# Moving part of the last gate's adaLN rows from the first product of an MLP into its second, as half rows through the weight loads' buffers

## The chip, the cores and the metric

The kernel runs on 1 core of one Trainium2 chip. The metric is device time in microseconds (us), the median over runs of one program. Before the change three runs took 1998.12, 2001.72 and 2003.39 us, so the median is 2001.72. One more execution was recorded by the profiler: it took 2001.01 us, with a span of 1999.3 us between its first and last recorded instruction.

The engines are named as the profile names them: PE multiplies matrices, DVE does elementwise arithmetic and sums along rows, ACT applies functions and copies, POOL and SP issue DMA transfers (SP issues most of them, in program order).

## The reference, cut to what matters

One decoder layer on x of shape (1, 512, 2048) in float32. A conditioning vector c gives six vectors of 2048 numbers, and the last of them, `gt2`, scales what the MLP adds at the end:

```python
c_act = jax.nn.silu(c.astype(jnp.float32))
mod = (c_act @ w_ada[l].astype(jnp.float32) + b_ada[l]).reshape(B, N_MOD, D)
sh1, sc1, gt1, sh2, sc2, gt2 = [mod[:, j][:, None, :] for j in range(N_MOD)]
# ... attention and a recurrence, then:
h = rmsnorm(x, g_norm_mlp[l]).astype(jnp.float32) * (1.0 + sc2) + sh2
hid = jnp.square(jax.nn.relu(jnp.einsum('bsd,df->bsf', h, w_mlp_in[l].astype(jnp.float32))))
y = jnp.einsum('bsf,fd->bsd', hid, w_mlp_out[l].astype(jnp.float32))
x = (x.astype(jnp.float32) + gt2 * y).astype(x.dtype)
```

`gt2` is a product of a vector of 2048 numbers with a 2048 x 2048 part of `w_ada`. It needs nothing but c and the weights, and it is needed first where the first 512 columns of the second MLP product are finished.

## The kernel before

All activations lie transposed, 128 features by 512 tokens to a tile. Each matrix product in float32 is made of three matmuls on operands that are split into a high and a low part (`h`, `lo`); the split of a weight is a copy on ACT (the high part) and a subtraction on DVE (the low part, line 122).

**The two MLP products** use one level of a Strassen scheme (function `strassen`): seven products of half-size blocks instead of eight. The work comes in *sets*. A set is one 512 KB weight load, the sums that Strassen needs of it, and 42 matmuls of 128 x 256 (seven products, two halves, three matmuls each; lines 1100 to 1102). The first product (8192 hidden features, 16 groups of 512) runs from group 1 on as 8 sets each; the second (`parts`, 13 pieces) has 124 sets of the same shape. In each set, function `operands`:

- SP loads the weights into one of three buffers with the tag `raw` (line 1056);
- DVE adds blocks of them (lines 1058, 1065, 1066) into a tile `ts`;
- ACT copies three raw blocks and the four sums into high parts (lines 1064 and 1070), and DVE subtracts for the low parts (line 122: `w<-raw` with 768 columns, `w<-ts` with 1024). The raw blocks' parts lie in six tiles `w3`, the sums' parts in five tiles (four `w4`, one `w5`), two tiles to a set. So the low part of a set's sums goes into the tile that held the high part of the set two before.

DVE and ACT execute in program order, and so does SP with its DMA issues. A raw buffer is free again when DVE's `w<-raw` of its set is done; the load three sets later waits for that on SP.

**Around the sets.** At the end of a group DVE combines the seven products from PSUM (`combine`, lines 1112 to 1118; ACT line 1111 copies the first one). In the first product DVE then makes four more sums of the result (line 946), ACT and DVE split it, and POOL writes all of it to DRAM (`keep_parts`). In the second product the results come back: five tiles of 256 KB for a set (`load_pair`, lines 1139 and 1142, on SP), and DVE finishes the split of two of five tiles (`split_pair`, line 122, `a<-a,a`). Those loads come in stretches, for four or eight sets on end. The time slots of `load_pair` and `split_pair` are set by the table `todo`.

**The rows of `gt2`** are made by `ada_late(GT2)`, a generator that runs beside the sets. It loads a quarter of 128 rows of the transposed `w_ada` (128 x 512, 256 KB, line 1190, on SP), and DVE multiplies it by the broadcast vector and sums along the row (line 1201, a SCALAR_TENSOR_TENSOR with a sum, followed by a DVE_READ_ACCUMULATOR); after four quarters two small operations (lines 1206 and 1207) add them into `mods`. That is 16 x 4 quarter rows. A generator in a `Lane` goes on when its `yield`s have counted down; `tick()` counts one for each set. Here `pace[0] = 1.9`, so a quarter row is due about every 1.9 sets, from group 2 on. The quarter rows lie in tiles with the tag `n` (five buffers, three loads ahead), the last two in tiles `a`. The list scheduler of the tile layer then places each instruction on its engine; instructions under `tc.high_priority` are moved ahead. Profile names drop buffer numbers, and both `w3`, `w4` and `w5` read `w` there.

Of the kernel before, what the change touches and what calls it, by code (L numbers as in the profile page):

```python
# [13 lines left out]
ALU = mybir.AluOpType  # L14
PSUM = bass.MemoryType.PSUM

P = 128
S = 512
D = 2048
NK = D // P  # L20
# [6 lines left out]
C_BADA = 0  # L27
# [37 lines left out]
def hybrid_layer_kernel(  # L65
# [13 lines left out]
    nc = tc.nc  # L79
# [18 lines left out]
    def T(tag, dt=F32, cols=None):  # L98
        return new(next(split_tag) if tag == "w4" else tag, dt, cols)
# [15 lines left out]
    tt = nc.vector.tensor_tensor  # L115
# [25 lines left out]
    cb = [T("cb"), T("cb")]  # L141
# [6 lines left out]
    def col(base, j):  # L148
        return vec[:, base + j : base + j + 1]
# [33 lines left out]
    def mod(m, j):  # L183
        return mods[:, m * NK + j : m * NK + j + 1]
# [256 lines left out]
    for o in range(8):  # L441
        t = T("a")
# [264 lines left out]
    pace = [3.2]  # L707
# [110 lines left out]
    def out_evac(outs, g, tok, held=None):  # L818
# [35 lines left out]
        out=gm2, in0=mods[:, SC2 * NK : (SC2 + 1) * NK], scalar=1.0, in1=vec[:, C_GMLP : C_GMLP + NK],  # L854
        op0=ALU.add, op1=ALU.mult,
# [325 lines left out]
        for f, p in todo.get(next(at), []):  # L1181
            f(p)

    LEAD, row = 3, ["n"]

    def ada_late(m):

        def load(i):
            t = T(row[0])
            tc.keep_in_program_order(nc.sync.dma_start(t, w_adaT[(m * NK + i // 4) * P : (m * NK + i // 4 + 1) * P, i % 4 * S : (i % 4 + 1) * S]))  # L1190
            return t

        ts = [load(i) for i in range(LEAD)]
        for i in range(4 * NK):
            t, q = ts.pop(0), i % 4
            if i + LEAD < 4 * NK:
                ts.append(load(i + LEAD))
            yield pace[0]
            if q == 0:
                ga = T("ga")  # L1200
            stt(
                out=t, in0=t, scalar=1.0, in1=cb[q // 2][:, q % 2 * S : (q % 2 + 1) * S], op0=ALU.mult, op1=ALU.mult,
                accum_out=ga[:, q : q + 1],
            )
            if q == 3:
                tt(out=ga[:, :2], in0=ga[:, :2], in1=ga[:, 2:4], op=ALU.add)
                stt(
                    out=mod(m, i // 4), in0=ga[:, 0:1], scalar=ga[:, 1:2], in1=col(C_BADA, m * NK + i // 4),
                    op0=ALU.add, op1=ALU.add,
                )  # L1210
        ready.add(m)

    pace[0] = 1.9
    w_pair = w_mlp_in.rearrange("(c k p) f -> k p c f", c=2, p=P)
    for g in range(1, NG):
        if g == 2:
# [8 lines left out]
        bg.add((keep_parts if g < NG - 2 else hold_parts)(g, *rs))  # L1225


    row[0] = "a"
    prodD = [[dp.tile([P, S], F32, name=f"prod_{n}_{i}") for i in range(7)] for n in range(NO)]
    w_blocks = w_mlp_out.rearrange("(g c b p) d -> g b p c d", c=2, b=2, p=P)  # L1230
    x2 = {}
# [235 lines left out]
```

## Time and profile before

| | before |
|---|---|
| median of three runs | 2001.72 us |
| the profiled execution | 2001.01 us |
| its span | 1999.3 us |
| PE busy | 1947.6 us (97%) |
| DVE busy | 1761.3 us (88%) |
| ACT busy | 1073.4 us (54%) |
| POOL busy | 193.6 us (10%) |
| granted PE clock, mean | 0.995 |
| DMA | 443.56 MB, 222 GB/s over the span |

Busy time counts an instruction from its start to its recorded end. Neighbours overlap on PE and DVE, so the time that one instruction costs is the distance between two starts, and the best measure of PE's progress is the number of matmuls that start in a stretch. In the span, the first MLP product's sets run from 764 to about 1363 us, the second product's until about 1959 us. Quarter rows run on DVE from 839.5 to 1359.2 us (62 of them), and two more after that.

### The profile page before, as it was taken

How to read it: one execution, taken by the hardware profiler on the slowest of the kernel's cores; microseconds unless marked ns; L12 is line 12 of the kernel's file. 1: busy time of each engine (PE TensorE's matmuls, PEld its weight loads, DVE VectorE, ACT ScalarE, POOL GpSimd, SP SyncE). 2: the span in 40 equal slices, each digit the busy share in tenths (PEclk: the TensorE clock that was granted, in tenths of full speed). 3: DMA queues.
4: the chain of work that ended last, by engine and by line, in shares of the span. 5: the costliest groups of instructions: out<-in, count | busy, mean ns of one | idle time of the engine just before them, and what ended most of it. 6: DMA issues, size and time to landing. Idle time of an engine off the chain costs nothing. (4 is left out here: it accounts for less than half of the span.)

```text
span 1999.3 us, 37951 instructions
## 1 busy us (share of the span) xinstructions
PE 1947.6 (97%) x14532; PEld 1836.1 (92%) x14532; DVE 1761.3 (88%) x2971; ACT 1073.4 (54%) x1572; POOL 193.6 (10%) x307
## 2 busy tenths in 40 slices
PE   8999999999999998999999999999999999999997
PEld 6789898788888898999999999999999999999996
DVE  8998786888998599999999999999879879878996
ACT  5443564786533386555556555555445645556552
POOL 0000000000000000111211211200110210211100
PEclk9999999999999999999999999999999999999998
DMA  9896655646779543766766765756567668679653
GB/s 365 305 319 213 201 169 183 188 140 213 228 251 362 183 144 113 236 211 196 227 201 191 227 204 187 232 170 219 190 232 270 226 246 287 215 253 346 225 196 111
DMA packets 205241, 443.56 MB, mean 222 GB/s; under 512 B 20481, under 2 KB 42113, under 8 KB 205058
## 3 DMA queue, kind: packets, MB, share of 16 engines
q1 hardware_dynamic: 176338, 356.58, 54.3%
q0 software_dynamic: 23680, 77.61, 10.4%
q10 hardware_dynamic: 5040, 6.93, 1.0%
q8 instruction: 114, 1.87, 0.4%
q14 instruction: 69, 0.57, 0.1%
HBM read 376.30 MB, written 64.75 MB: 221 GB/s over the span
## 5 line engine op out<-in xcount | busy, mean ns | idle before, releaser
L1100 PE MATMUL ps_mm<-a,w 128*128 128x256 f32 x1696 | 468.3, 277 | 3.0 <-DVE a L1112 1.2
L1102 PE MATMUL ps_mm<-a,w 128*128 128x256 f32 x1696 | 468.5, 277 | 0.4 <-DVE w L122 0.3
L1101 PE MATMUL ps_mm<-a,w 128*128 128x256 f32 x1696 | 468.3, 276 | 0.3 <-DVE a L122 0.3
L1070 ACT ACTIVATE w<-ts 128x1024 fp32r<-128x1024 f32 x244 | 258.4, 1059 | 276.2 <-DVE ts L1066 246.5
L1102 PE MATMUL ps_z<-a,w 128*128 128x256 f32 x1304 | 361.6, 278 | 7.0 <-DVE w L122 6.7
L1100 PE MATMUL ps_z<-a,w 128*128 128x256 f32 x1304 | 361.6, 278 | 3.8 <-DVE a L1116 1.7
L1101 PE MATMUL ps_z<-a,w 128*128 128x256 f32 x1304 | 360.9, 277 | 0.1
L122 DVE TENSOR_TENSOR w<-ts,w 128x1024 fp32r<-128x1024 f32 x244 | 298.4, 1223 | 54.7 <-PE ps_mm L1101 17.7
L1100 PEld LDWEIGHTS ps_mm<-a,w 128*128 128x128 f32 x1696 | 318.3, 188 | 4.3 <-issue 2.6
L1102 PEld LDWEIGHTS ps_mm<-a,w 128*128 128x128 f32 x1696 | 318.4, 188 | 1.2 <-DVE w L122 1.0
L1101 PEld LDWEIGHTS ps_mm<-a,w 128*128 128x128 f32 x1696 | 318.5, 188 | 0.7 <-DVE a L122 0.7
L122 DVE TENSOR_TENSOR w<-raw,w 128x768 fp32r<-128x768 f32 (+1 forms) x296 | 268.5, 908 | 37.1 <-ACT w L244 21.8
L1064 ACT ACTIVATE w<-raw 128x768 fp32r<-128x768 f32 x244 | 204.4, 838 | 168.4 <-issue 77.2
L1102 PEld LDWEIGHTS ps_z<-a,w 128*128 128x128 f32 x1304 | 245.6, 189 | 8.4 <-DVE w L122 8.3
L1100 PEld LDWEIGHTS ps_z<-a,w 128*128 128x128 f32 x1304 | 245.6, 188 | 5.4 <-issue 2.2
L1101 PEld LDWEIGHTS ps_z<-a,w 128*128 128x128 f32 x1304 | 245.6, 188 | 0.6 <-DVE a L122 0.6
L244 ACT ACTIVATE wh<-wr 128x512 fp32r<-128x512 f32 (+1 forms) x184 | 113.1, 618 | 151.3 <-PE ps_mm L262 62.4
L1058 DVE TENSOR_TENSOR ts<-raw 128x512 f32<-128x512 f32 x244 | 167.6, 688 | 14.1 <-DMA raw<-in_w_mlp_out_dram 13.6
L259 PE MATMUL ps_mm<-a,wh 128*128 128x512 f32 x448 | 176.3, 394 | 3.8 <-ACT wh L244 2.2
L263 PE MATMUL ps_mm<-a,wl 128*128 128x512 f32 x448 | 175.4, 392 | 0.8 <-DVE wl L122 0.6
L262 PE MATMUL ps_mm<-a,wh 128*128 128x512 f32 x448 | 174.8, 390 | 0.0
L211 DVE SCALAR_TENSOR_TENSOR x<-x,cb 128x1024 f32<-128x1024 f32 x108 | 131.8, 1224 | 25.0 <-DMA x<-in_w_adaT_dram 24.9
(336 smaller groups left out, 4156.7 us busy)
## 6 DMA issues: line engine op xcount, KB each, us to landing
raw<-in_w_mlp_out_dram SPq DMA_DIRECT2D x124, 512.0 KB, 4.7
raw<-in_w_mlp_in_dram SPq DMA_DIRECT2D x120, 512.0 KB, 3.9
x<-in_w_adaT_dram SPq DMA_DIRECT2D x108, 512.0 KB, 5.9
wr<-in_w_in_dram SPq DMA_DIRECT2D x160, 256.0 KB, 3.4
tt<-in_w_adaT_dram SPq DMA_DIRECT2D x52, 512.0 KB, 6.4
part<-a POOLq DMA_DIRECT2D x84, 256.0 KB, 3.9
a<-part SPq DMA_DIRECT2D x84, 256.0 KB, 6.4
prod<-a POOLq DMA_DIRECT2D x63, 256.0 KB, 5.7
```

Source lines behind the costliest of these rows:

```text
L122: tt(out=out, in0=full, in1=f32(high), op=ALU.subtract)
L211: ins = stt(out=t, in0=t, scalar=1.0, in1=cb[q_], op0=ALU.mult, op1=ALU.mult, accum_out=self.ga[:, q_ : q_ + 1],)
L244: act(h[:, :n], r[:, :n], AF.Copy)
L259: first = mm(out, wh, ah, start=start, stop=False, **kw)
L262: mm(out, wh, al, start=False, stop=False, **kw)
L263: mm(out, wl, ah, start=False, stop=stop, **kw)
L1058: tt(out=t[:, : 2 * HT].rearrange("p (a b) -> p a b", a=2), in0=r[:, HT : 3 * HT].rearrange("p (a b) -> p a b", a=2), in1=r[:, q_(0)].unsq ...
L1064: act(h, r[:, HT:], AF.Copy)
L1070: act(h, t, AF.Copy)
L1100: mm(out, wh[:, blk(i)], ah, start=st, stop=False, **kw)
L1101: mm(out, wh[:, blk(i)], al, start=False, stop=False, **kw)
L1102: mm(out, wl[:, blk(i)], ah, start=False, stop=j == js[-1], **kw)
```

## The change

The rows of `gt2` become due every 3.0 sets in place of 1.9. From the start of the second product on (`wide`), what is not yet loaded comes as half rows (128 x 1024, 512 KB, line 1197 of the changed file), one every 6 sets, in the three `raw` buffers of the weight loads and under the same priority as these; DVE works on a half row in one instruction (line 1207 of the changed file), about two sets after its load is placed.

```diff
-    LEAD, row = 3, ["n"]
+    LEAD, wide = 3, []
...
+        def load(n, at):
+            i, c0 = divmod(at, 2048)
+            src = w_adaT[(m * NK + i) * P : (m * NK + i + 1) * P, c0 : c0 + n]
+            if n == S:
+                t = T("n")
+                tc.keep_in_program_order(nc.sync.dma_start(t, src))
+            else:
+                with tc.high_priority(offset=SETW):
+                    t = T("raw")
+                    nc.sync.dma_start(t, src)
+            return t, n, at
...
+        def dot(t, n, at):
+            c0 = at % 2048
+            if c0 == 0:
+                used.clear()
+                used.append(T("ga"))
+            ga, q = used[0], len(used) - 1
+            used.append(n)
             stt(
-                out=t, in0=t, scalar=1.0, in1=cb[q // 2][:, q % 2 * S : (q % 2 + 1) * S], op0=ALU.mult, op1=ALU.mult,
+                out=t, in0=t, scalar=1.0, in1=cb[c0 // 1024][:, c0 % 1024 : c0 % 1024 + n], op0=ALU.mult, op1=ALU.mult,
                 accum_out=ga[:, q : q + 1],
             )
...
+        used, ts, at, end = [], [], 0, 2048 * NK
+        while at < end or ts:
+            while at < end and len(ts) < LEAD and not (wide and at % 1024 == 0):
+                ts.append(load(S, at))
+                at += S
+            if ts:
+                yield pace[0]
+                dot(*ts.pop(0))
+            else:
+                t = load(1024, at)
+                at += 1024
+                yield 2.0
+                with tc.high_priority(offset=SETW):
+                    dot(*t)
+                del t
+                yield 2 * pace[0] - 2.0
...
-    pace[0] = 1.9
+    pace[0] = 3.0
...
-    row[0] = "a"
+    wide.append(1)
```

In the built program this makes 40 quarter rows and 12 half rows (40 x 512 + 12 x 1024 = 16 x 2048 columns). All 40 quarter rows now stand on DVE before the last combination of the first product; before, 62 stood there and 2 after it. The orders of PE and ACT differ only around the end of the first product and, on ACT, by a few places of split copies in the second; POOL's is the same, and before group 2 and after the last half row nothing is moved.

On DVE, the end of group 3 of the first product, just ahead of its combination (the third L1112, into `ps_o`). `n` is a quarter row, `ga` its sums, `ts` and `w` belong to sets. Before:

```order
L1058 TENSOR_TENSOR ts_9520<-raw_9518 128x512
L946 TENSOR_TENSOR a_8981<-a_8981,a_9255 128x512
L1065 TENSOR_TENSOR ts_9520<-ts_9520,raw_9518 128x256
L1201 SCALAR_TENSOR_TENSOR n_8979,ga_9136<-n_8979,cb_82 128x512
L1066 TENSOR_TENSOR ts_9520<-ts_9520,raw_9518 128x256
L1206 TENSOR_TENSOR ga_9136<-ga_9136 128x2
L1201 SCALAR_TENSOR_TENSOR n_9138,ga_9654<-n_9138,cb_81 128x512
...
L1065 TENSOR_TENSOR ts_9592<-ts_9592,raw_9590 128x256
L1201 SCALAR_TENSOR_TENSOR n_9259,ga_9654<-n_9259,cb_81 128x512
L1066 TENSOR_TENSOR ts_9592<-ts_9592,raw_9590 128x256
L1201 SCALAR_TENSOR_TENSOR n_9378,ga_9654<-n_9378,cb_82 128x512
```

After:

```order
L1058 TENSOR_TENSOR ts_9507<-raw_9505 128x512
L1207 SCALAR_TENSOR_TENSOR n_9250,ga_9426<-n_9250,cb_82 128x512
L1065 TENSOR_TENSOR ts_9507<-ts_9507,raw_9505 128x256
L1207 SCALAR_TENSOR_TENSOR n_9428,ga_9426<-n_9428,cb_82 128x512
L1066 TENSOR_TENSOR ts_9507<-ts_9507,raw_9505 128x256
L1213 TENSOR_TENSOR ga_9426<-ga_9426 128x2
L1207 SCALAR_TENSOR_TENSOR n_9642,ga_10213<-n_9642,cb_81 128x512
...
L1058 TENSOR_TENSOR ts_9579<-raw_9577 128x512
L1214 SCALAR_TENSOR_TENSOR mods<-ga_9426,vec 128x1
L1065 TENSOR_TENSOR ts_9579<-ts_9579,raw_9577 128x256
L1066 TENSOR_TENSOR ts_9579<-ts_9579,raw_9577 128x256
```

Four quarter rows stood in the last two sets of this group, now three, and none in the last set. Up to this place stood 11 quarter rows, now 9; up to the end of group 4 it is 18 and 12. In each later group up to the 14th stood 4 or 5, now 2 or 3.

On SP, the first stretch of pair loads in the second product. Before:

```order
L1056 DMA raw_17788<-in_w_mlp_out_dram 128x2x512
L1139 DMA a_17652<-part_6510 128x512
L1142 DMA a_17656<-sum_6526 128x512
L1142 DMA a_17657<-sum_6526 128x512
L1139 DMA a_17716<-part_6510 128x512
L1056 DMA raw_17860<-in_w_mlp_out_dram 128x2x512
L1139 DMA a_17717<-part_6510 128x512
```

After, at the same pair loads:

```order
L1056 DMA raw_17714<-in_w_mlp_out_dram 128x2x512
L1139 DMA a_17578<-part_6510 128x512
L1142 DMA a_17582<-sum_6526 128x512
L1142 DMA a_17583<-sum_6526 128x512
L1139 DMA a_17642<-part_6510 128x512
L1197 DMA raw_17786<-in_w_adaT_dram 128x1024
L1139 DMA a_17643<-part_6510 128x512
L1139 DMA a_17644<-part_6510 128x512
L1142 DMA a_17648<-sum_6526 128x512
L1142 DMA a_17649<-sum_6526 128x512
L1056 DMA raw_17788<-in_w_mlp_out_dram 128x2x512
L1056 DMA raw_17860<-in_w_mlp_out_dram 128x2x512
```

The half row takes the place of a weight load, and this and every later weight load until the half row is used stand one raw buffer later.

On DVE at the same place, after the change (`a<-a,a` are the split subtractions; the first of them in this stretch stood right behind the same `ts<-raw` before):

```order
L122 TENSOR_TENSOR w_2969_17657<-raw_17652,w_2968_17656 128x768
L1058 TENSOR_TENSOR ts_17716<-raw_17714 128x512
L1207 SCALAR_TENSOR_TENSOR raw_17786,ga_17922<-raw_17786,cb_81 128x1024
L1065 TENSOR_TENSOR ts_17716<-ts_17716,raw_17714 128x256
L122 TENSOR_TENSOR a_17390<-a_17390,a_17708 128x512
L1066 TENSOR_TENSOR ts_17716<-ts_17716,raw_17714 128x256
L122 TENSOR_TENSOR a_17391<-a_17391,a_17711 128x512
L122 TENSOR_TENSOR w_2971_17663<-ts_17654,w_2970_17662 128x1024
```

The half row stands ahead of the rest of its set, and the next three sets hold two split subtractions each where the first two held three each and the third one. Of the twelve half rows two stand in this stretch (at its start and at its end) and two in the second stretch.

More of the change, by code (lines that the diff above doesn't have):

```diff
@@ L1182, in after_set @@
             f(p)
-    LEAD, row = 3, ["n"]
+    LEAD, wide = 3, []
     def ada_late(m):
[L1188 to L1200, printed above, removed]
+        def load(n, at):
[16 more added lines that the diff above has]
+            used.append(n)
@@ L1201, in ada_late @@
             stt(
-                out=t, in0=t, scalar=1.0, in1=cb[q // 2][:, q % 2 * S : (q % 2 + 1) * S], op0=ALU.mult, op1=ALU.mult,
+                out=t, in0=t, scalar=1.0, in1=cb[c0 // 1024][:, c0 % 1024 : c0 % 1024 + n], op0=ALU.mult, op1=ALU.mult,
                 accum_out=ga[:, q : q + 1],
             )
-            if q == 3:
-                tt(out=ga[:, :2], in0=ga[:, :2], in1=ga[:, 2:4], op=ALU.add)
+            if c0 + n == 2048:
+                if q > 1:
+                    tt(out=ga[:, : q - 1], in0=ga[:, : q - 1], in1=ga[:, 2 : q + 1], op=ALU.add)
@@ L1207, in ada_late @@
                 stt(
-                    out=mod(m, i // 4), in0=ga[:, 0:1], scalar=ga[:, 1:2], in1=col(C_BADA, m * NK + i // 4),
+                    out=mod(m, at // 2048), in0=ga[:, 0:1], scalar=ga[:, 1:2], in1=col(C_BADA, m * NK + at // 2048),
                     op0=ALU.add, op1=ALU.add,
                 )
+        used, ts, at, end = [], [], 0, 2048 * NK
[14 more added lines that the diff above has]
+                yield 2 * pace[0] - 2.0
```

## The prediction, as put on record before the change was run

> **What bounds the kernel now.** I read the page's totals first, then PE by stretches, then who PE waits for, then DVE's instructions one by one.
>
> ```profile
> span 1999.3 us, 37951 instructions
> PE 1947.6 (97%) x14532; PEld 1836.1 (92%) x14532; DVE 1761.3 (88%) x2971; ACT 1073.4 (54%) x1572; POOL 193.6 (10%) x307
> ```
>
> PE leaves about 52 us in all, and much of that lies where nothing is changed. In the windows view (span, then busy time and instructions of PE, PEld, DVE, ACT, POOL, clock, DMA share, GB/s) the third column's count is what to look at:
>
> ```profile
> 850.00:950.00 100.00, 97.22 (x836) 95.47 (x835) 98.80 (x179) 54.48 (x75) 17.00 (x25) 1.00 0.64 204
> 950.00:1150.00 200.00, 199.91 (x1763) 199.74 (x1763) 197.47 (x337) 111.19 (x146) 38.88 (x57) 1.00 0.66 212
> 1150.00:1350.00 200.00, 198.15 (x1740) 197.46 (x1740) 196.90 (x336) 110.03 (x148) 30.04 (x45) 1.00 0.62 198
> 1350.00:1400.00 50.00, 46.99 (x396) 45.64 (x395) 48.13 (x79) 30.22 (x44) 0.56 (x1) 1.00 0.61 218
> 1400.00:1480.00 80.00, 80.00 (x709) 80.00 (x708) 67.51 (x103) 38.06 (x47) 11.25 (x21) 1.00 0.49 166
> 1480.00:1530.00 50.00, 50.00 (x444) 50.00 (x443) 43.16 (x66) 26.74 (x36) 2.18 (x4) 1.00 1.00 370
> 1640.00:1690.00 50.00, 50.00 (x444) 50.00 (x443) 45.30 (x69) 28.43 (x38) 0.00 (x0) 1.00 0.95 342
> ```
>
> In the second product PE starts 709 matmuls in 80 us, 8.86 per us, without a gap: 42 of a set take 4.74 us. In the first product DVE is busy 98 to 99% and PE falls behind: 50 matmuls of 886 in the first row (5.6 us), 9 (1.0 us), 32 (3.6 us), and 48 (5.4 us) at the change of products. The first three sum to 10.2 us. So the first product has two engines at their limit, the second only PE. What PE waits for, from 840 to 1345 us and from 1345 to 1410 us:
>
> ```profile
> PE ps_z L1100 <- DVE a L1116: 1.7, 3, 0.6
> PE ps_mm L1100 <- DVE a L1116: 0.9, 2, 0.6
> PE ps_o L1100 <- DVE a L1112: 0.5, 1, 0.5
> ...
> PE ps_z L1100 <- ACT a L1111: 1.4, 1, 1.4
> PE ps_mm L1100 <- DVE a L1112: 1.2, 1, 1.2
> ```
>
> These are combinations at the ends of groups: PE needs the PSUM bank, and DVE, which works in order, reaches the combination late.
>
> **First product: quarter rows removed.** On DVE, start by start, in group 3:
>
> ```profile
> 885.48 0.70 DVE L1201 SCALAR_TENSOR_TENSOR n<-n,cb 128x512 f32<-128x512 f32 x1
> 886.09 0.10 DVE L1201 DVE_READ_ACCUMULATOR n<-n,cb 128x1 f32 x1
> 886.09 0.43 DVE L1066 TENSOR_TENSOR ts<-ts,raw 128x256 f32<-128x256 f32 x1
> 886.42 0.17 DVE L1206 TENSOR_TENSOR ga<-ga 128x2 f32<-128x2 f32 x1
> 886.50 0.70 DVE L1201 SCALAR_TENSOR_TENSOR n<-n,cb 128x512 f32<-128x512 f32 x1
> 887.11 0.10 DVE L1201 DVE_READ_ACCUMULATOR n<-n,cb 128x1 f32 x1
> 887.11 1.24 DVE L122 TENSOR_TENSOR w<-ts,w 128x1024 fp32r<-128x1024 f32 x1
> 888.24 0.97 DVE L122 TENSOR_TENSOR w<-raw,w 128x768 fp32r<-128x768 f32 x1
> 889.11 0.70 DVE L1058 TENSOR_TENSOR ts<-raw 128x512 f32<-128x512 f32 x1
> 889.71 0.23 DVE L1207 SCALAR_TENSOR_TENSOR mods<-ga,vec 128x1 f32<-128x1 f32 x1
> 889.84 0.43 DVE L1065 TENSOR_TENSOR ts<-ts,raw 128x256 f32<-128x256 f32 x1
> ```
>
> A quarter row holds DVE for 0.61 us (885.48 to 886.09; reading the sum is hidden), the end of a row for 0.08 + 0.13 us, so 0.66 us each. The order has 22 fewer of them ahead of the last combination (62 to 40): 14.5 us of DVE time. PE can only get back what it loses. By the end of group 4 (about 939 us) six are gone, 4.0 us, and of the first row's 5.6 us I take 4.0. Behind it 16 more go, 10.6 us against 4.6 us lost; I take 3.8, since part of a combination's wait is its own length. Together 7.8 us. Bounds: 4.5 us, the idle time that the seven rows of the waits view from 840 to 1345 us sum to (the three largest stand above), and 10.2 us, the whole loss.
>
> **Change of products.** PE loses 5.4 us there, 2.6 us of it as the two recorded waits, behind weight loads that share SP with the first pair loads. Two quarter loads of 256 KB leave this place (0.5 MB at the 370 GB/s of the loaded stretch, 1.4 us) and two quarter rows leave DVE (1.3 us). I take 1.5 us of gain; bounds 0 and 2.6.
>
> **Second product: half rows.** No half row exists in the trace. DVE's nearest row of that length is the 1024-wide subtraction, 1.13 us from start to start (887.11 to 888.24); I take that, with the end of a row 1.2 us, for 12 half rows. The two quarter rows that stood here fall away (1.3 us, hidden). What hides the half rows is DVE's lead. Its idle time from 1400 to 1700 us:
>
> ```profile
> L122 DVE TENSOR_TENSOR w<-ts,w 128x1024 fp32r<-128x1024 f32 x64 | 78.3, 1223 | 28.6 <-PE ps_mm L1102 11.5 <-PE ps_mm L1101 9.7 <-PE ps_z L1101 4.5
> L1058 DVE TENSOR_TENSOR ts<-raw 128x512 f32<-128x512 f32 x64 | 43.9, 686 | 7.6 <-DMA raw<-in_w_mlp_out_dram 7.5
> ```
>
> 28.6 us is DVE waiting for PE to free a `w` tile: it is as far ahead as five tiles allow. The low part waits for PE's last use of the set two before, so DVE leads by one set (4.74 us) and PE's first eight matmuls (0.9 us), less its own 1.13 us: about 4.5 us. In quiet stretches a half row fits in that: eight of twelve cost nothing.
>
> The four others lie in or beside the two stretches of pair loads. Median time to landing of a weight load from 1400 to 1480, 1480 to 1530 and 1640 to 1690 us (last column), then DVE's first instruction of successive sets, and a load on SP:
>
> ```profile
> raw<-in_w_mlp_out_dram SPq DMA_DIRECT2D x17, 512.0 KB, 3.8
> ...
> raw<-in_w_mlp_out_dram SPq DMA_DIRECT2D x11, 512.0 KB, 6.1
> ...
> raw<-in_w_mlp_out_dram SPq DMA_DIRECT2D x10, 512.0 KB, 6.1
> ...
> 1484.29 0.69 DVE L1058 TENSOR_TENSOR ts<-raw 128x512 f32<-128x512 f32 x1
> 1491.25 0.69 DVE L1058 TENSOR_TENSOR ts<-raw 128x512 f32<-128x512 f32 x1 [2.12 <-DMA raw<-in_w_mlp_out_dram]
> 1496.37 0.69 DVE L1058 TENSOR_TENSOR ts<-raw 128x512 f32<-128x512 f32 x1 [1.50 <-DMA raw<-in_w_mlp_out_dram]
> 1500.94 0.69 DVE L1058 TENSOR_TENSOR ts<-raw 128x512 f32<-128x512 f32 x1 [0.96 <-DMA raw<-in_w_mlp_out_dram]
> 1506.03 0.68 DVE L1058 TENSOR_TENSOR ts<-raw 128x512 f32<-128x512 f32 x1
> 1511.12 0.69 DVE L1058 TENSOR_TENSOR ts<-raw 128x512 f32<-128x512 f32 x1
> 1528.94 0.68 DVE L1058 TENSOR_TENSOR ts<-raw 128x512 f32<-128x512 f32 x1
> ...
> 1498.34 0.38 SPq L1056 DMA_DIRECT2D raw<-in_w_mlp_out_dram  x1
> ```
>
> Already now DVE waits there for loads that were placed three buffers ahead. From 1484.29 to 1511.12 it makes five sets in 26.83 us where PE needs 23.7: it falls back 3.1 us of its 4.5, and PE feels nothing (444 matmuls). By 1528.94 it has regained some: nine sets in 44.65 us against 42.7, 2.0 us behind. Now the half row takes a buffer, so each load around it is placed one set later. The first half row has the place of the load at 1498.34 and lands, at 6.1 us, at 1504.4; DVE comes to it at 1501.55 (1500.94 and 0.61) and stands for 2.9 us with all of its set's subtractions queued behind. Then 1.2 us of work, and the load two behind has one set of DVE time (5.1 us, 1506.03 to 1511.12) for 6.1 us: 1.0 us. Sum 5.1 us. The second half row, at the end of the stretch, has 3.9 us between the freeing of its buffer and its use (0.60 + 0.35 + 0.33 + 1.13 + 0.87 + 0.60), against a landing between 3.8 and 6.1 us: 1.1 us of wait, 1.2 of work, 2.3. Lag 2.0 + 5.1 + 2.3 = 9.4 us, less 4.5: PE loses 4.9 us. In the second stretch the last half row falls behind the pair loads and is free; the other costs 2.2 (6.1 less 3.9) + 1.2 + 1.0 = 4.4, and 2.0 + 4.4 - 4.5 = 1.9 us. Together 6.8 us. Bounds: 0, if the half rows land in time (1.2 us each fits into the 1.4 us left), and 20 us, if all four hold DVE as long as the first, and two weight loads more wait behind each.
>
> The Trainium skill, page "DMA: Bandwidth & Descriptors", section "Queues, rings and completion order", says that each DMA engine consumes one queue's descriptors in ring order, so a half row waits for the pair loads that SP issued before it; the trace agrees, with 6.1 us in the stretches against 3.8 us outside. Its section "Anatomy of one DMA — SWDGE (gpsimd) path" gives 2.0 us and bytes over 436 GB/s: an estimate of 3.2 us for 512 KB, fitted on another queue. By that figure alone no half row would be late, and the sum would come to the first rival's time; the trace's 6.1 us decides against it.
>
> **Sum.** -7.8 - 1.5 + 6.8 = -2.5 us against the profiled execution's 2001.01 us: 1998.5 us. The median stood 0.7 us above that execution, so I forecast **1999.2 us**.
>
> **Rivals.** (1) *The half rows are hidden.* For it: DVE has 12.5 of 80 us idle in the quiet stretch, and the order moves split subtractions of the stretch behind the first half row (two and two where three and three stood, 1.2 us of relief). Against it: three waits for loads in the rows above, with the full three buffers. Then only 7.8 + 1.5 = 9.3 us of gain are left: 1992.4 us.
>
> (2) *Buffers starve, slower.* The raw buffers become the bound of the stretches: four half rows cost 7 us of DVE each (1.2 of work, a landing 3 us later than the median, the load two behind late by as much), 28 + 2 x 2.0 - 2 x 4.5 = 23 us, net +14 us: 2015 us. It decides as soon as the four average 3.6 us (4 x 3.6 + 4.0 - 9.0 = 9.4 us, the gain). For it: DMA is full at 370 GB/s and half rows add bytes. Against it: 0.5 MB is 1.4 us, and when PE stalls the loads catch up.
>
> (3) *The first product gives nothing back.* The combinations' waits end with instructions of the combination itself (L1116), so a DVE that comes earlier may wait for ACT's copy instead. Then only the change of products and, at most, the 1.0 us of the row from 950 to 1150 come back: +6.8 - 1.5 - 1.0, about 2006 us. Against it: stalls are largest where six or seven quarter rows stand in a group.
>
> **How the numbers follow.** Forecast 0.45, (1) 0.32, (2) 0.13, (3) 0.10. I hold 0.3% (6.0 us) for what a measurement can tell from no change. Faster by more than that: nearly all of (1) and a little of the forecast's lower side, 0.35. Slower by more: most of (2) and a third of (3), 0.14. Within: 0.51. The forecast's own range is 1994 to 2005; with (1) below and the near part of (2) above, 1990.5 to 2007 holds 8 in 10.
>
> **What would show it.** Right: matmul counts of 870 or more in 100 us from 850 to 950, near 8.86 per us until 1350, DVE busy around 95% there; a new idle time on DVE ahead of L1207 on half rows, ended by DMA from `in_w_adaT_dram`, in the two stretches alone; PE waits on `w L122` there, which do not exist now. PE counts of 444 in both stretches would show (1) right; waits on raw loads in quiet stretches too would show (2); combinations that still stop PE by the same 4.5 us would show (3). A loss at another place, behind 1740 us or before 800, would prove the whole account wrong, since nothing is moved there.

## The result

The changed kernel took 2006.72 us in the median of 20 runs (1999.42 to 2012.88), the kernel before 2001.91 us in 20 runs on the same chip (1998.12 to 2007.38). The ratio is 1.002 with a 95% interval of 1.0011 to 1.0029: slower by 0.2%, where 1999.2 us, slightly faster, was forecast. The profiled execution took 2003.67 us (span 2001.9 us) against 2001.01 us (span 1999.3 us) before: 2.6 us of span are there to be explained. The median of the changed kernel lies 3.1 us above its profiled execution, and of that part there is no trace. In all that follows, the ratios leave out four executions (2141 to 5026 us) that ran far longer than the others of their kernel.

### The profile page after: what moved, and what is told of

It is laid out like the page before. It is cut to its first block, busy times and chain, and to the rows that moved or that the text cites. A ratio compares the mean times of both kernels' runs of the same rounds, so it can differ in the third digit from the quotient of the medians.

```text
span 2001.9 us, 37893 instructions
## 1 busy us (share of the span) xinstructions
PE 1946.2 (97%) x14532; PEld 1836.8 (92%) x14532; DVE 1761.4 (88%) x2941; ACT 1076.6 (54%) x1572; POOL 193.6 (10%) x307
## 5 line engine op out<-in xcount | busy, mean ns | idle before, releaser
L122 DVE TENSOR_TENSOR wl<-wr,wh 128x512 fp32r<-128x512 f32 (+1 forms) x184 | 124.5, 679 | 33.1 <-ACT wh L244 32.3
```

The costliest lines, as they stand in the source:

```text
L122: tt(out=out, in0=full, in1=f32(high), op=ALU.subtract)
```

## The profile after

The windows view of the changed kernel, with the columns of the prediction (the third is PE's busy time with the count of matmuls):

```profile
850.00:950.00 100.00, 99.25 (x872) 98.92 (x871) 98.57 (x170) 57.47 (x78) 18.45 (x28) 1.00 0.61 195
950.00:1150.00 200.00, 200.00 (x1767) 200.00 (x1767) 194.72 (x319) 110.43 (x144) 36.13 (x53) 1.00 0.63 201
1150.00:1350.00 200.00, 200.00 (x1767) 200.00 (x1766) 195.03 (x321) 114.43 (x151) 30.04 (x44) 1.00 0.63 202
1345.00:1410.00 65.00, 60.82 (x502) 59.42 (x500) 61.63 (x98) 36.64 (x53) 3.76 (x7) 0.97 0.55 194
1480.00:1530.00 50.00, 47.74 (x420) 47.53 (x420) 40.20 (x61) 25.10 (x34) 0.99 (x2) 1.00 0.96 344
1530.00:1640.00 110.00, 108.36 (x951) 107.77 (x950) 91.75 (x137) 60.27 (x80) 19.52 (x36) 1.00 0.64 224
1640.00:1690.00 50.00, 48.60 (x428) 48.41 (x427) 44.71 (x71) 25.94 (x34) 0.00 (x0) 1.00 0.97 347
1690.00:1740.00 50.00, 49.51 (x437) 49.31 (x436) 42.58 (x64) 27.18 (x35) 6.50 (x12) 1.00 0.57 202
```

And the stretches of the kernel before that the prediction did not show:

```profile
1345.00:1410.00 65.00, 61.99 (x528) 60.64 (x528) 63.13 (x101) 38.12 (x54) 3.77 (x7) 1.00 0.66 227
1530.00:1640.00 110.00, 110.00 (x973) 110.00 (x972) 88.14 (x128) 59.94 (x80) 19.50 (x36) 1.00 0.59 204
1690.00:1740.00 50.00, 50.00 (x444) 50.00 (x443) 40.51 (x59) 25.67 (x34) 6.51 (x12) 1.00 0.55 190
```

A matmul that runs across the border of two windows counts in both, so counts are compared window by window. At 8.86 matmuls per us: from 850 to 1345 us PE starts 4357 matmuls where it started 4291, 7.5 us gained. At the change of products it has 502 for 528, 2.9 us lost, and in that row the clock is 0.97, not 1.00. From 1410 to 1740 us the five windows sum to 2856 for 2925 (620 in the first 70 us in both), 7.8 us lost: 24 and 16 matmuls in the two stretches of pair loads (4.5 us), 22 and 7 in what follows them (3.3 us). Together 29 matmuls, 3.3 us, for 2.6 us of span.

PE's new stops behind the end of the first product, in its timeline (the bracket is the recorded idle time and who ended it; one of 0.34 us, ended by ACT, is left out):

```profile
1393.84 0.39 PE L1101 MATMUL ps_mm<-a,w 128*128 128x256 f32 x1 [2.08 <-DVE a L122]
1504.11 0.39 PE L1102 MATMUL ps_o<-a,w 128*128 128x256 f32 x1 [2.26 <-DVE w L122]
1533.23 0.39 PE L1102 MATMUL ps_o<-a,w 128*128 128x256 f32 x1 [0.17 <-DVE w L122]
1556.48 0.38 PE L1100 MATMUL ps_mm<-a,w 128*128 128x256 f32 x1 [0.73 <-ACT ps_mm L1090]
1595.60 0.38 PE L1100 MATMUL ps_z<-a,w 128*128 128x256 f32 x1 [0.74 <-ACT ps_z L1090]
1651.26 0.39 PE L1102 MATMUL ps_mm<-a,w 128*128 128x256 f32 x1 [1.40 <-DVE w L122]
1712.43 0.38 PE L1100 MATMUL ps_z<-a,w 128*128 128x256 f32 x1 [0.49 <-ACT ps_z L1090]
```

Four of them end with a subtraction on DVE. The others end with line 1090, ACT's copy of reloaded partial products into PSUM; ACT in turn waited 2.01, 2.15 and 1.28 us there for the reload to land, and in the kernel before 0.30, 0.42 and 0.44 us. The first stop stands at the change of products, where the prediction had a gain. DVE there:

```profile
1387.20 0.68 DVE L122 TENSOR_TENSOR a<-a,a 128x512 fp32r<-128x512 f32 x1
1387.81 0.42 DVE L1065 TENSOR_TENSOR ts<-ts,raw 128x256 f32<-128x256 f32 x1
1388.14 0.69 DVE L122 TENSOR_TENSOR a<-a,a 128x512 fp32r<-128x512 f32 x1
1388.74 0.42 DVE L1066 TENSOR_TENSOR ts<-ts,raw 128x256 f32<-128x256 f32 x1
1389.08 1.22 DVE L1207 SCALAR_TENSOR_TENSOR raw<-raw,cb 128x1024 f32<-128x1024 f32 x1
1390.22 0.08 DVE L1207 DVE_READ_ACCUMULATOR raw<-raw,cb 128x1 f32 x1
1390.22 2.36 DVE L122 TENSOR_TENSOR w<-ts,w 128x1024 fp32r<-128x1024 f32 x2
1392.49 0.69 DVE L1058 TENSOR_TENSOR ts<-raw 128x512 f32<-128x512 f32 x1
1393.10 0.69 DVE L122 TENSOR_TENSOR a<-a,a 128x512 fp32r<-128x512 f32 x1
```

Three splits of `a` belong together. In the kernel before, each follows the last by 0.9 us:

```profile
1397.11 0.69 DVE L122 TENSOR_TENSOR a<-a,a 128x512 fp32r<-128x512 f32 x1
1397.71 0.42 DVE L1065 TENSOR_TENSOR ts<-ts,raw 128x256 f32<-128x256 f32 x1
1398.04 0.69 DVE L122 TENSOR_TENSOR a<-a,a 128x512 fp32r<-128x512 f32 x1
1398.64 0.42 DVE L1066 TENSOR_TENSOR ts<-ts,raw 128x256 f32<-128x256 f32 x1
1398.98 0.69 DVE L122 TENSOR_TENSOR a<-a,a 128x512 fp32r<-128x512 f32 x1
```

Now the first half row stands between them, and behind it two long subtractions and a sum: 4.96 us from the second split to the third, for which PE waits. PE went on until 1391.76 us (1393.84 less 2.08). With the half row alone in between, the third split would have stood 1.14 us later than in the kernel before, at about 1390.2, and would have ended at about 1390.9, ahead of that; this is an estimate from the rows shown. It took the half row and the subtractions together.

The stretches show what the prediction described: DVE stands, in order, for a half row that lands late, twice for over 3 us.

```profile
1499.81 1.23 DVE L1207 SCALAR_TENSOR_TENSOR raw<-raw,cb 128x1024 f32<-128x1024 f32 x1 [3.25 <-DMA raw<-in_w_adaT_dram]
1529.40 1.23 DVE L1207 SCALAR_TENSOR_TENSOR raw<-raw,cb 128x1024 f32<-128x1024 f32 x1 [0.61 <-DMA raw<-in_w_adaT_dram]
1648.03 1.23 DVE L1207 SCALAR_TENSOR_TENSOR raw<-raw,cb 128x1024 f32<-128x1024 f32 x1 [3.47 <-DMA raw<-in_w_adaT_dram]
1674.78 1.23 DVE L1207 SCALAR_TENSOR_TENSOR raw<-raw,cb 128x1024 f32<-128x1024 f32 x1 [0.57 <-DMA raw<-in_w_adaT_dram]
```

## The experiments

All runs but quiet, which stands below, in one table: the ratio to the kernel before, run beside each on the same chip, with its interval, and the counts of matmuls from one profiled execution each. The column "rest" is 1410 to 1740 us without the two stretches. A hundred matmuls are 11.3 us. A profiled execution need not be a middle one: in first_low it was the longest of twelve (2003.79 us, median 1992.97).

| kernel | ratio (95%) | 850-1345 | 1345-1410 | 1480-1530 | 1640-1690 | rest | sum |
|---|---|---|---|---|---|---|---|
| before | 1 | 4291 | 528 | 444 | 444 | 2037 | 7744 |
| changed | 1.0020 (1.0011-1.0029) | 4357 | 502 | 420 | 428 | 2008 | 7715 |
| no_late | 0.9967 (0.9954-0.9980) | 4345 | 539 | 444 | 444 | 2037 | 7809 |
| first_moved | 1.0011 (1.0000-1.0022) | 4349 | 531 | 402 | 429 | 1981 | 7692 |
| bursts_moved | 0.9975 (0.9962-0.9988) | 4351 | 491 | 443 | 444 | 2029 | 7758 |
| quiet_again | 0.9969 (0.9957-0.9981) | 4357 | 542 | 444 | 439 | 2013 | 7795 |
| quiet_p4 | 0.9970 (0.9958-0.9981) | 4370 | 544 | 444 | 444 | 1988 | 7790 |
| load_only | 0.9990 (0.9980-0.9999) | 4360 | 533 | 406 | 440 | 2004 | 7743 |
| half_in_a | 1.0045 (1.0027-1.0062) | 4353 | 535 | 381 | 376 | 1957 | 7602 |
| raw4 | 1.0052 (1.0035-1.0070) | 4303 | 533 | 430 | 428 | 2010 | 7704 |
| quarters_a | 1.0011 (0.9999-1.0023) | 4326 | 533 | 393 | 423 | 2015 | 7690 |
| quiet_loads | 0.9954 (0.9940-0.9969) | 4362 | 538 | 444 | 443 | 2027 | 7814 |
| quiet_work | 0.9971 (0.9960-0.9981) | 4358 | 541 | 443 | 439 | 2018 | 7799 |
| quiet_wait | 0.9995 (0.9986-1.0004) | 4351 | 542 | 429 | 412 | 2019 | 7753 |
| change_work | 0.9965 (0.9951-0.9979) | 4356 | 535 | 443 | 444 | 2014 | 7792 |
| first_low | 0.9966 (0.9955-0.9977) | 4332 | 530 | 444 | 444 | 2025 | 7775 |
| all_low | 0.9995 (0.9984-1.0006) | 4363 | 536 | 423 | 435 | 2006 | 7763 |

### What thinning alone is worth

**no_late**, from the kernel before:

```diff
+        end = 40
...
-        for i in range(4 * NK):
+        for i in range(end):
...
-            if i + LEAD < 4 * NK:
+            if i + LEAD < end:
...
-    pace[0] = 1.9
+    pace[0] = 3.0
```

> The kernel before with quarter rows due every 3.0 sets, and the last 24 quarter rows (the last six blocks of 128 values of gt2) left out of the work; a copy of others stands in their place. It shows what thinning alone is worth, with nothing in the second product. Theory: the first product gives back 7.5 us (4357 matmuls or more from 850 to 1345 us) and the change of products about 1.5: about 1993 us. Rival: what PE gets back in the first product is lost again at the next thing it must wait for (the change of products loses more because DVE and PE arrive there in another order): 1997 us or more, and a change of products that loses 8 us, not 4.

Measured: 0.9967, 6.6 us of gain, with PE at full rate in all of the second product. The first product's gain is real and is not taken back at the change of products (539 matmuls, not fewer than 528). The forecast of 7.8 + 1.5 us for these two was too much by 2.7 us, just outside the interval (4.0 to 9.2 us).

### Where the half rows stand

Three kernels replace the even spacing of the half rows by a list of distances in sets. The rest of the changed kernel stays.

```diff
             else:
+                yield gaps.pop(0)
                 t = load(1024, at)
                 at += 1024
                 yield 2.0
                 with tc.high_priority(offset=SETW):
                     dot(*t)
                 del t
-                yield 2 * pace[0] - 2.0
...
+        gaps = [6.0, 4.0, 1.0, 1.0, 4.0, 4.0, 4.0, 4.0, 4.0, 4.0, 4.0, 4.0]       # first_moved
+        gaps = [0.0, 4.0, 1.0, 1.0, 1.0, 1.0, 16.0, 1.0, 1.0, 4.0, 17.0, 1.0]     # bursts_moved
+        gaps = [4.0, 0.0, 2.0, 1.0, 20.0, 0.0, 3.0, 1.0, 3.0, 17.0, 3.0, 1.0]     # quiet
```

> Only the first of the twelve half rows is moved, from the eighth set of the second product (the change of products) to its 23rd set, a quiet stretch. Theory: in the changed kernel the first half row stands on DVE ahead of two subtractions and of a split of a; PE stops 2.3 us behind it and then runs 3.3 us at half the granted clock (15 matmuls at 0.21 instead of 0.113 us, 1.6 us). Without it 1345 to 1410 us has about 535 matmuls instead of 502 and the time falls by about 3.9 us against the changed kernel's 2006.7 us, to about 2003 us. Rival: the loss there comes from the pair loads, which now stand earlier on SP because no quarter rows lie between them; then it stays, about 2006.5 us, and PE's wait on the split of a stays too.

> The half rows that stood in the two stretches of pair loads (sets 32, 38, 62, 68 of the second product) stand in quiet stretches (sets 17, 23, 47, 78), and the last but one is moved from 74 to 75; the first stays at set 8. Theory: PE's waits on the low part of the sums in the stretches (2.4 + 0.3 + 1.6 us) go, and the waits for reloaded partial products that follow them (2.5 us in three places) go at least in part: 4.3 to 6.8 us less than the changed kernel, 2000 to 2002.5 us. Rival: a half row costs the same wherever it stands, since what it costs is DVE's 1.2 us and one weight buffer; then nothing is gained, about 2006.5 us, with waits in the quiet stretches instead.

> All twelve half rows stand in quiet stretches, at sets 12, 14, 18, 21, 43, 45, 50, 53, 58, 77, 82, 85 of the second product; none stands in the change of products or in a stretch of pair loads, and none within two sets ahead of the end of a piece but two. Theory: both losses go, 3.9 + 4.3 to 6.8 us: 1996 to 1998.5 us, faster than the kernel before by 3.5 to 6 us, and 1410 to 1740 us has 2905 matmuls or more. Rival (a half row costs the same everywhere): about 2006.5 us.

Measured: without the half row at set 8 the change of products has 531 matmuls (changed: 502), as expected, but the stretches lose more than in the changed kernel (402 matmuls for 420 in the first), so the time falls only to 1.0011. Without the half rows in the stretches these have 443 and 444, and the time falls to 0.9975, although the change of products still loses (491). With both, the median of quiet was 1996.0 us against 2000.6 us; its interval (0.9968 to 1.0008) is wide and reaches past 1. So quiet was run again:

> The kernel quiet once more, unchanged: in its first comparison the interval was wide (0.9968 to 1.0008) because one execution ran at a granted clock of 0.945 throughout. With a median of 1996.0 us against 2000.6 us there, a ratio of 0.9977 is expected, with an interval below 1; if the half rows in quiet stretches cost something after all, 0.999 or more.

Measured: 0.9969. The rows of `gt2` that are moved then cost little: no_late, which leaves them out, stands at 0.9967, though in the two traces quiet_again starts 29 matmuls fewer from 1410 to 1740 us. DVE stands for half rows in quiet_again too, in four places of its quiet stretches. The longest wait, and PE behind it:

```profile
1554.90 1.23 DVE L1207 SCALAR_TENSOR_TENSOR raw<-raw,cb 128x1024 f32<-128x1024 f32 x1 [2.31 <-DMA raw<-in_w_adaT_dram]
1558.13 0.38 PE L1102 MATMUL ps_mm<-a,w 128*128 128x256 f32 x1 [0.71 <-DVE w L122]
```

Behind the other three (0.90, 1.21 and 1.56 us) PE does not wait for DVE at all. Both losses of the changed kernel are for the most part a matter of where the half rows stand, and quiet beats the kernel before and the changed one.

**quiet_p4** goes further in the same direction (`pace[0] = 4.0` and a longer list of distances: 32 quarter rows in the first product and 16 half rows, 4, 8 and 4 of them in the three quiet stretches where quiet has 4, 5 and 3):

> Quarter rows every 4.0 sets in the first product in place of 3.0 (about 30 in place of 40), and so 17 half rows in the second product, all in quiet stretches from set 19 on. If the first product still loses by DVE's queue at 3.0 (863 to 878 matmuls of 886 from 850 to 950 us, 1 to 2.6 us), about 1 us more is gained than with quiet, ratio 0.997; if five more half rows in quiet stretches cost DVE's lead more than that, 0.998 to 1.000.

Measured: 0.9970, the same. The first product is at full rate (PE is busy in all of the 495 us, 4370 matmuls), but the column "rest" now lacks 49 matmuls (1988 for 2037; quiet_again lacks 24), some of them at half clock behind one stop. Here DVE waits longer for a half row, and PE stops for longer:

```profile
1593.12 1.23 DVE L1207 SCALAR_TENSOR_TENSOR raw<-raw,cb 128x1024 f32<-128x1024 f32 x1 [4.35 <-DMA raw<-in_w_adaT_dram]
1596.35 0.56 PE L1102 MATMUL ps_mm<-a,w 128*128 128x256 f32 x1 [2.23 <-DVE w L122]
```

### What of a half row costs

Four kernels change what a half row is made of.

```diff
 load_only
-                out=t, in0=t, scalar=1.0, in1=cb[c0 // 1024][:, c0 % 1024 : c0 % 1024 + n], op0=ALU.mult, op1=ALU.mult,
+                out=t[:, : min(n, S) // (1 if n == S else 4)], in0=t[:, : min(n, S) // (1 if n == S else 4)], scalar=1.0,
+                in1=cb[c0 // 1024][:, c0 % 1024 : c0 % 1024 + (n if n == S else P)], op0=ALU.mult, op1=ALU.mult,
 half_in_a
-                    t = T("raw")
-                    nc.sync.dma_start(t, src)
+                    t = [T("a"), T("a")]
+                    for i, u in enumerate(t):
+                        nc.sync.dma_start(u, src[:, i * S : (i + 1) * S])
...
-                    dot(*t)
+                    for i, u in enumerate(t[0]):
+                        dot(u, S, t[2] + i * S)
 raw4
-BUFS = {"cb": 2, "a": 64, "ga": 2, "n": 5}
+BUFS = {"cb": 2, "a": 62, "ga": 2, "n": 5}
-    "sums": ("right", {"ts": 2, "raw": 3, "w4": 4}),
+    "sums": ("right", {"ts": 2, "raw": 4, "w4": 4}),
 quarters_a (from the kernel before)
-    pace[0] = 1.9
+    pace[0] = 3.0
```

(load_only sums 128 columns of a half row; quarter rows stay whole.)

> The changed kernel with DVE summing only the first 128 of the 1024 columns of each half row: the loads, their places and the weight buffers they take stay, DVE's 1.14 us falls to about 0.2 us (the rest of the sums for those rows is left out of the work). Theory for the change of products: it is DVE's 1.14 us ahead of the split of a that stops PE; 1345 to 1410 us then has 530 matmuls or more (502 in the changed kernel, 539 without any rows). Theory for the stretches: the half row still holds a weight buffer and DVE still stands until it has landed, so most of their loss (4.3 us) stays, and the ratio is about 0.9995. Rival: DVE's time explains both, all losses go, ratio 0.997.

> The changed kernel with each half row loaded as two quarter rows into two tiles with the tag a (64 buffers) in place of one weight buffer, at the same places and priority, and DVE working on them one behind the other (1.2 us for two). Theory that the weight buffer is what costs: the stretches of pair loads have 440 matmuls or more each, and the waits for reloaded partial products shrink; with the loss at the change of products still there (the DVE time of the first pair of quarter rows is the same, about 40 matmuls) the ratio to the kernel before is about 0.998. Rival, that DVE's time is what costs: the waits on the low part of the sums stay as they were (4.3 us), and the ratio stays at 1.001 or more.

> The changed kernel with four weight buffers in place of three, paid for with two of the 64 a tiles. Half rows and DVE's work on them stay as they are. Theory that a half row costs because it takes one of three buffers: no wait on loads in the two stretches, PE counts of 440 or more in both, the loss at the change of products unchanged; ratio about 0.998. Rival, DVE's time: ratio 1.001 or more with the same waits. Beside it two a tiles fewer may hold back pair loads, which would show as waits on a tiles.

> The kernel before with one number changed: quarter rows every 3.0 sets in place of 1.9. What is left for the second product comes as quarter rows in a tiles as in the kernel before, 24 of them, one by one. Theory: DVE's lead takes 0.66 us at a time nearly everywhere; the first product's gain stays (7.5 us), the change of products loses about 5 us as before or a little more, the stretches lose 0 to 2: ratio 0.9975 to 0.9985, as good as half rows in quiet stretches, without touching the weight buffers. Rival: any row in the change of products and in the stretches costs PE its whole DVE time there (about 11 of them, 7 us): ratio 1.000 or more.

Measured: my expectation for the weight buffer fell, and quarters_a, expected at 0.9975 to 0.9985, came out at 1.0011. With tiles of their own (half_in_a, quarters_a) and with a fourth buffer (raw4) the first stretch still loses 63, 51 and 14 matmuls of 444, and DVE stands longer for the row than in the changed kernel. Its first instruction on a row in the first stretch, in load_only, half_in_a, raw4 and quarters_a:

```profile
1494.46 0.29 DVE L1207 SCALAR_TENSOR_TENSOR raw<-raw,cb 128x128 f32<-128x128 f32 x1 [3.48 <-DMA raw<-in_w_adaT_dram]
```

```profile
1485.74 0.69 DVE L1208 SCALAR_TENSOR_TENSOR a<-a,cb 128x512 f32<-128x512 f32 x1 [9.03 <-DMA a<-in_w_adaT_dram]
```

```profile
1504.12 1.23 DVE L1207 SCALAR_TENSOR_TENSOR raw<-raw,cb 128x1024 f32<-128x1024 f32 x1 [5.79 <-DMA raw<-in_w_adaT_dram]
```

```profile
1488.41 0.69 DVE L1201 SCALAR_TENSOR_TENSOR a<-a,cb 128x512 f32<-128x512 f32 x1 [8.67 <-DMA a<-in_w_adaT_dram]
```

What they share is the load that DVE stands for. load_only, with almost no DVE time, stands as long (3.48 us) and loses 38 there, some of them to the half clock described at the end. raw4 does not compare as a whole: with a weight buffer more and two `a` tiles fewer it has 54 matmuls fewer in the first product. At the change of products all four have 533 to 535, but they differ in the order there. In half_in_a and quarters_a the rows stand behind the splits of `a`. In load_only the shortened row stands ahead of the third split, but no other subtraction does, and the split follows the second by 1.14 us. In raw4 the whole half row and one `w<-ts` stand ahead of it, 4.15 us from split to split, and PE stops for only 0.26 us: a place ahead of the split need not cost much, it depends on how far the split is pushed and on when PE needs it.

### Bytes, time or waiting

Three kernels start from quiet, whose stretches are clean, and add one property of a half row each, in the sets 32, 38, 62 and 68.

```diff
 quiet_loads
     def operands(src):
         with tc.high_priority(offset=SETW):
+            nset[0] += 1 if wide else 0
+            if wide and nset[0] in IN_STRETCH:          # (32, 38, 62, 68)
+                for i in range(2):
+                    nc.sync.dma_start(T("a"), w_adaT[GT2 * NK * P : (GT2 * NK + 1) * P, i * S : (i + 1) * S])
 quiet_work (behind the subtraction of the raw blocks)
+            if wide and nset[0] in IN_STRETCH:
+                g = T("ga")
+                for i in range(2):
+                    stt(out=T("a"), in0=t[:, i * S : (i + 1) * S], scalar=1.0, in1=cb[i][:, :S], op0=ALU.mult, op1=ALU.mult, accum_out=g[:, i : i + 1])
 quiet_wait (quiet_loads, its two tiles kept in the list seen_, and two sets later)
+            if seen_ and nset[0] - 2 in IN_STRETCH:
+                g = T("ga")
+                for i in range(2):
+                    tt(out=g[:, i : i + 1], in0=seen_[i][:, :1], in1=cb[0][:, :1], op=ALU.mult)
```

> The kernel with all half rows in quiet stretches (quiet), and at sets 32, 38, 62, 68 of the second product, where the changed kernel has half rows, two more loads of 256 KB each into a tiles that nobody reads: the bytes of a half row in the stretches of pair loads, without a weight buffer, without DVE's work and without a wait of DVE on them. Theory, that PE stops because DVE, which works in order, stands for a half row that lands late: DVE never stands for these, and the stretches keep 440 matmuls or more; ratio as quiet's, about 0.998. Rival, that the bytes themselves cost (each 0.5 MB is 1.4 us at 370 GB/s, and the weight loads behind come later by that): the stretches lose about 15 to 25 matmuls each (2 to 3 us), ratio 1.0005 or more.

> The kernel quiet, and in the sets 32, 38, 62, 68 of the second product two more products with a sum of 128 x 512 on DVE, on that set's own sums (1.2 us together, results unused): the DVE time of a half row in the stretches without its load. Theory of the late half row: DVE's lead takes 1.2 us, the stretches keep 440 matmuls or more, ratio as quiet's. Rival, that DVE's time is what costs: PE waits on the low part of the sums there, each row about 1 us, 4 us in all, ratio 1.000.

> The kernel quiet_loads, with two multiplications of one column (128 x 1) on DVE that read the two unused loads, at the place where the changed kernel has its half row: right behind the first sum of a set whose weights SP loaded just ahead. It adds DVE's wait for these loads, and almost no DVE time. Theory of the late load: DVE stands some 3 us at the first read of each stretch (3.25 us in the changed kernel), PE stops for 1.5 to 3 us on the low part of the sums behind it, and the stretches lose 10 to 40 matmuls together against quiet_loads (444 and 443); ratio 0.997 to 0.9985 against quiet_loads' 0.9954. Rival, that only the sum of wait, DVE time and a taken weight buffer costs: 440 or more in both stretches, and a ratio of 0.9955 to 0.9965.

Measured: the bytes alone leave both stretches full (444 and 443), DVE's time alone too (443 and 439, the same as quiet_again's 444 and 439). Reads of one column, which do little but wait, cost 15 and 31 matmuls, 5.2 us, and take the ratio from 0.9954 to 0.9995, more than expected. In the second stretch of quiet_wait, DVE and then PE:

```profile
1653.77 0.16 DVE L1064 TENSOR_TENSOR ga<-a,cb 128x1 f32<-128x1 f32 x1 [6.91 <-DMA a<-in_w_adaT_dram]
```

```profile
1655.99 0.38 PE L1114 MATMUL ps_mm<-a,w 128*128 128x256 f32 x1 [2.63 <-DVE w L122]
```

So in the stretches the wait is enough by itself. (That quiet_loads is a little faster than quiet lies within the two intervals; I draw nothing from it.)

### Order or time at the change of products

```diff
 change_work (from quiet_work)
-    nset, IN_STRETCH = [0], (32, 38, 62, 68)
+    nset, IN_STRETCH = [0], (10,)
 first_low (from bursts_moved)
-                with tc.high_priority(offset=SETW):
+                with tc.high_priority(offset=SETW if len(gaps) < 11 else 0):
                     dot(*t)
 all_low (from the changed kernel)
-                with tc.high_priority(offset=SETW):
-                    dot(*t)
+                dot(*t)
```

> The kernel quiet, with two products with a sum of 128 x 512 on DVE (1.2 us, results unused, no load) added in the tenth set of the second product, where DVE works on the changed kernel's first half row. Theory that at the change of products DVE has no lead and its time is what costs: 1345 to 1410 us has 500 to 530 matmuls (quiet: 542), with a PE wait on the split of a or on the low part of the sums of 1 us or more; ratio 0.998 to 0.999. Rival, that it was the place of the half row in DVE's order, ahead of the split of a, and not its time: 538 or more, ratio as quiet's 0.997.

> The kernel bursts_moved, with DVE's work on the first half row alone placed without the raised priority: the load stays at the eighth set, DVE works on it 16 instructions later, behind all three splits of a and their subtractions, which stand next to each other again. Theory of the order: PE's wait of 2.35 us on the split of a and the half clock behind it go, 1345 to 1410 us has 530 matmuls or more (bursts_moved: 491), and the ratio falls from bursts_moved's 0.9975 to about 0.996. Rival, that the half row's time costs wherever it stands at the change of products: 510 or fewer, ratio 0.9975.

> The changed kernel without the raised priority on DVE's work on the half rows; loads, buffers and their priority stay. In the order this moves five of the twelve half rows on DVE: the first by 16 instructions, behind the splits of a, those of the two stretches by 8 to 16 (a set or two), the quiet ones not at all. Theory (a late load on which DVE stands in order, and the split of a pushed back): DVE no longer stands 3 us for the half rows of the stretches, both have 440 matmuls or more, the change of products 530 or more, and the ratio falls from 1.002 to about 0.997. Rival, that a half row takes one of three weight buffers, now for longer: DVE stands for weight loads instead, the stretches lose as much as now or more, ratio 1.000 to 1.003.

Measured: 1.2 us more of DVE at the change of products, behind the splits, leave 535 matmuls of 542 and no change of the time (0.9965). The half row itself, loaded where bursts_moved loads it but worked on behind the three splits, brings the count from 491 to 530 and the ratio from 0.9975 to 0.9966; the intervals overlap, the stop is gone. First bursts_moved's stop, then DVE in first_low, where PE has no stop:

```profile
1392.71 0.39 PE L1101 MATMUL ps_mm<-a,w 128*128 128x256 f32 x1 [2.10 <-DVE a L122]
```

```profile
1391.48 0.68 DVE L122 TENSOR_TENSOR a<-a,a 128x512 fp32r<-128x512 f32 x1
...
1392.41 0.68 DVE L122 TENSOR_TENSOR a<-a,a 128x512 fp32r<-128x512 f32 x1
...
1393.35 0.68 DVE L122 TENSOR_TENSOR a<-a,a 128x512 fp32r<-128x512 f32 x1
...
1406.82 1.22 DVE L1207 SCALAR_TENSOR_TENSOR raw<-raw,cb 128x1024 f32<-128x1024 f32 x1
```

So it was the place in the order, not the time: the rival that was written for change_work holds.

all_low recovers the change of products (536) and brings the ratio from 1.0020 to 0.9995, but the stretches stay as they were. There the second theory shares with its rival: DVE no longer stands at the half row in the first stretch, but at the weights. The half row holds its buffer for longer, 16.7 us from load to work (1485.19 to 1501.84) against 6.5 us in the changed kernel (1493.27 to 1499.81). That this is why the weights come late follows from the order of the loads; no run isolates it.

```profile
1496.15 0.69 DVE L1058 TENSOR_TENSOR ts<-raw 128x512 f32<-128x512 f32 x1 [3.18 <-DMA raw<-in_w_mlp_out_dram]
```

## Why the prediction was wrong, and where it was right

**First product.** Forecast 7.8 us back, measured 7.5. The counts came as foretold (872 in the first 100 us, then 1767 in 200). Only "DVE around 95%" was off: it was busy for 488.3 of the 500 us, 97.7%. Rival (3) is out.

**Change of products: the step that failed.** "I take 1.5 us of gain; bounds 0 and 2.6" became a loss of 2.9 us, an error of 4.4 us, which is enough to turn the sign: with 1.5 us of gain the counts would sum to 1.2 us of gain. The step priced the two quarter loads that leave and not the half row that arrives, which "eight of twelve cost nothing" had put among the free ones. Without it the place does gain: 530 to 544 matmuls for 528 in the ten kernels that have no half row there or have it behind the splits (no_late, first_moved, the five that begin with quiet, change_work, first_low, all_low), 0.2 to 1.8 us. What the half row cost there was neither of the items that I had for a half row by itself (1.2 us of work, a late landing). Its raised priority put it ahead of a split that PE needs next, and two more raised subtractions went ahead of that split with it, 4.96 us where it had been 0.9; PE stopped for 2.08 us. With the row behind the splits the stop is gone (first_low, 530 matmuls against 491 in bursts_moved). The order of the change shows this; I read it for the stretches only. A part of the loss I had no term for at all, the half clock behind the stop (below).

**Second product.** Forecast 6.8 us, measured 7.8. The mechanism was right in the stretches: waits of 3.25, 0.61, 3.47 and 0.57 us stood where 2.9, 1.1, 2.2 and 0 were worked out. The second stretch lost 1.8 us (forecast 1.9), the first 2.7 (forecast 4.9: mis-sized by 2.2). The mis-sized term is the second half row's 2.3 us. By the same sum the first half row alone takes 2.0 + 5.1 - 4.5 = 2.6 us from PE, and its stop is 2.26 us; behind the second stands one of 0.17 us (1533.23). The 3.3 us outside the stretches were forecast as zero, and this is the second step that failed. PE's recorded stops there end, but for those 0.17 us, with line 1090: 1.96 us in three places, where ACT waits for reloads that land late. Such waits came in most kernels with half rows and not in no_late; what makes the reloads late I did not isolate. That the total (7.8 against 6.8) came near is partly luck: 2.2 us too much in one place and 3.3 us that were missed in another.

**The rivals.** Rival (1), half rows hidden, 1992.4 us: not what this change did, but what its parts can do; quiet, first_low and change_work stand at 0.9965 to 0.9969, 1995 us by the kernel before. Rival (2), starving buffers, is not it as written: DVE's waits and work at the four half rows come to 12.5 us (7.9 + 4 x 1.14), not 28, and with a fourth buffer, in raw4, the stretches still lose 14 and 16 matmuls. In all_low, where the half row is held longer, DVE does wait for the weights instead.

**Sum.** -7.5 + 2.9 + 7.8 = +3.2 us in the profile, against -2.5 forecast. The medians lie 4.8 us apart; what the unprofiled executions add is not shown.

## What to carry to other kernels

Work that fills an in-order engine's spare time is free here only as far as its wait and its work fit into the engine's lead. In the stretches neither its bytes alone nor its 1.2 us alone cost anything, while reads of one column behind late loads cost 5 us; in quiet stretches PE did not feel waits of up to 1.56 us, and stopped for 0.71 us behind one of 2.31 us and for 2.23 us behind one of 4.35 us. So place the load well ahead, or the reader behind the late stretch, and do not give filler work the priority of the work it is to hide behind: it can push something that is needed next. And read the new order at every place where the moved work arrives, not only where you expect trouble.

## What I had not expected of the hardware

**A short stop of PE can be followed by half speed.** In the changed kernel, right behind the stop at 1393.84 us, the granted clock falls to a half; from 1394.53 to 1397.94 us 17 matmuls start 0.21 us apart in place of 0.113. In the windows view:

```profile
1394.00:1396.00 2.00, 2.00 (x12) 2.00 (x13) 1.31 (x3) 1.33 (x3) 1.32 (x3) 0.63 0.13 51
1396.00:1398.00 2.00, 2.00 (x12) 2.00 (x11) 1.96 (x4) 0.76 (x2) 1.78 (x4) 0.51 0.93 342
```

About 1.6 us (3.41 for 16 distances, less 16 x 0.113) on top of a stop of 2.08 us. In bursts_moved it came behind the stop of 2.10 us at the same place. In first_moved it came after both stops of 2.73 us, for 5.9 us at the second; that stop in PE's timeline, and the windows behind it:

```profile
1710.57 0.58 PE L1100 MATMUL ps_z<-a,w 128*128 128x256 f32 x1 [2.73 <-ACT ps_z L1090]
```

```profile
1712.00:1714.00 2.00, 2.00 (x12) 2.00 (x11) 1.23 (x1) 1.09 (x2) 0.89 (x2) 0.50 1.04 405
1714.00:1716.00 2.00, 2.00 (x11) 2.00 (x11) 1.66 (x3) 1.22 (x2) 0.00 (x0) 0.50 1.00 395
```

It did not come after the changed kernel's longer stop at 1504.11 us (2.26 us), nor after 2.63 us in quiet_wait. So it is not the length alone that decides. The Trainium skill, page "TensorE: Matmul & The Clock Gate", section "Part 1: The HAM clock gate (the "warmup" mystery)", tells of a free-running window of about 3.4 us, and of a fall after an idle window of that length. Here stops of 2.1 us were enough, so the traces are consistent with a window that does not follow the kernel (a longer stop, no fall) but not with an idle window of that length as the condition, and there the measurement decides. No run here changes the phase on purpose; that the spread of the changed kernel's runs (1999.4 to 2012.9 us, against 1991.5 to 1997.3 us in quiet_again) comes from it is only argued.
